# Two-layer hybrid backbone on one core: order ties in retention and feed-forward, and one output row tile moved to SBUF

## The chip, the cores and the metric

The kernel runs on one core of a Trainium2 chip. Five engines work side by side: TensorE (PE in the profile; PEld is its weight load), VectorE (DVE), ScalarE (ACT), GpSimd (POOL) and SyncE (SP), which here only issues DMAs. The metric is the device time of one execution in microseconds; the median of several runs counts.

## The reference, cut to what matters

Two layers work on 512 latent tokens and 256 context tokens of width 1024. Layer 0 is windowed attention plus a SwiGLU feed-forward and is not touched here. Layer 1 is bidirectional retention with four heads, again followed by a feed-forward. For latent tokens, each head computes

```python
q, k = rope_2d(h_x @ w_q), rope_2d(h_x @ w_k)         # 256 columns a head
v, g = h_x @ w_v, h_x @ w_g                           # 512 columns a head
k_c, v_c = h_c @ w_k, h_c @ w_v                       # 256 context tokens
o = retention(q, k, v, k_c, v_c, decay)               # both directions
y = (o - mean(o)) * rsqrt(var(o) + EPS) * gn_gain     # over the head's 512 columns
out += (silu(g) * y) @ w_o
```

and the feed-forward computes `(silu(h @ w_gate) * (h @ w_up)) @ w_out` with 2816 hidden columns.

## The kernel before, in words

**Products in two halves.** Every float32 operand is split into a high part (a cast to the matmul's type, on ScalarE, line 164) and a low part (the rest, on VectorE, line 165). A product is three matmuls: high by high, low by high, high by low. So each weight chunk of 128 x 1024 costs one DMA (lines 122 and 1204), one cast and one subtraction before TensorE can use it. Raw chunks lie in two buffers, `wraw`, or in four wide ones, `wx`.

**Fewer products by sums.** The projections of layer 1 use a seven-product scheme for 2 x 2 blocks. Sums of weight chunks are made on VectorE (lines 1416 to 1420, 1453, 1538 in retention; 903 to 906 in the feed-forward, in `quarter_sums`) or by an accumulating DMA of GpSimd (`add_chunk`, line 1208).

**One retention head.** The loop `for hd in range(RH)` runs: first key products; context keys in PSUM tile `kc` (`context_keys` splits them into `rkc`, lines 1407 to 1411); the query products; `rope_pair` for queries and for keys (lines 1300 to 1311: two products, a sum at line 1307, then a split); value and gate products into the two PSUM banks `Z`; then `scores(m)` for six blocks of 128 keys (lines 1496 to 1515), four latent and two context. A block's score goes to PSUM tile `pj`, is multiplied by the decay strip on VectorE (line 1512, called the shaping here) into `hn`, and is split into `wx`; `accumulate(m)` (lines 1517 to 1522) multiplies it into four PSUM row tiles `ov`, two in the banks `X` and two in the banks `Y`. Each row tile holds 128 tokens by 512 columns. While these run, the gate's weights come in: two weight sums `w1` (line 1538) and two plain chunks `w22` (line 1540). Then every row tile is normalised in place (line 1566), multiplied by the gate (`gated`, line 1572), transposed on TensorE (line 1583) into four tiles in the same banks `X` and `Y`, and copied out with its gain (`turned`, a ScalarE copy at line 1588 and a VectorE low part at line 1589). `out_tile` (line 1619) multiplies by the output weights and adds to the stream.

In head 0 some things differ: in the list `lows` stand the low parts of two weight chunks (`w3`); the casts of two more chunks (`w4`) and the low parts of the context keys are tied behind the last key split (`rope_end`).

In the last head the output is done by halves of 256 tokens. Tokens 256 to 511 (row tiles 2 and 3) are transposed first, the others between output tiles. Squares of the stream are summed there for the second norm, whose logarithm and exponential need another table of ScalarE than the gate's SiLU. `ln_exp_turn()` places that table's load and keeps it as `turn["pre"]`. `second_norm` makes the feed-forward's operand `hx`; `first_weights` brings in its first weights (lines 1643 and 1644).

**The feed-forward.** Hidden tiles come one by one, numbered `f`. The first three are made plainly, the others by `seven`. After the first tile of every group, `output` multiplies the group before by its output weights: one PSUM tile `pj` (of two) for each of eight column blocks, added to the stream on VectorE (line 256). `first_adds` holds the first two of these additions, `copies` the ScalarE copies of the last `seven` (lines 1745 and 1747).

**What sets the order.** Instructions are ordered for each engine when the program is built, by a list scheduler with its own estimate of times and with program order as priority. `after(ins, others)` adds an edge that only this scheduler sees: `ins` is placed after `others`, with no wait on the chip. On the chip each engine takes its instructions in the order so fixed, and waits in place for the data of the next one.

Of the kernel before, what the change touches and what calls it, by code (L numbers as in the profile page):

```python
# [49 lines left out]
def dit_kernel(ctx, tc, xT, cT, crow, small, consts, masks, tabs0, tabs1, jtab, adaQ, adaN, adaT, wst, out):  # L50
    nc = tc.nc
# [610 lines left out]
    vt = []  # L662
# [236 lines left out]

    def quarter_sums(g, u, behind=()):  # L900
# [4 lines left out]
        nc.vector.tensor_tensor(u[:, r_], u[:, r_], g[:, l_], op=sub)  # L905
        nc.vector.tensor_tensor(g[:, r_], g[:, r_], u[:, r_], op=sub)
# [393 lines left out]
    def rope_pair(o, cos1, sin1, behind=()):  # L1300

        res = []
        for op, f0, f1 in ((sub, cos1, sin1), (add, sin1, cos1)):
            a, b = t_hn(SX), t_sq(SX)
            after(nc.vector.tensor_tensor(a, o[0], f0, op=mult), behind)
            after(nc.vector.tensor_tensor(b, o[1], f1, op=mult), behind)
            rope_sum[0] = nc.vector.tensor_tensor(a, a, b, op=op)
# [58 lines left out]
    for hd in range(RH):  # L1366
# [93 lines left out]
        else:  # L1460
# [7 lines left out]
            qh = rope_pair(qt, cos1, sin1, ready)  # L1468
            for low in lows:
                after(low, rope_sum)  # L1470
        kh = rope_pair(kt, cos1, sin1)
        while strip_sums:
            after(strip_sums.pop(), rope_sum)
        if hd == 0:
            context_keys()
        gate = [T(qa, 512, "gate", 4) for _ in range(4)]
# [6 lines left out]
        if hd == 0:  # L1483
            w4 = [split_chunk(v, rope_end) for v in v11]

        def last_values(t):
# [9 lines left out]
        def scores(m):  # L1496
# [3 lines left out]
            v = T(qw, 1024, "wx", 4, F32R)  # L1500
            after(split(vt[m], v[:, 0:512], v[:, 512:]), [] if hd else rope_end)
            so = pj()
# [8 lines left out]
            dec_ap = dx[:, 384 - 128 * mm:896 - 128 * mm] if s == 0 else dcx[:, 128 - 128 * mm:640 - 128 * mm]  # L1511
            nc.vector.scalar_tensor_tensor(sd, so, 1.0 / 16.0, dec_ap, mult, mult)
            ss = T(qw, 1024, "wx", 4, F32R)
# [3 lines left out]
        def accumulate(m, v, sc):  # L1517
            for n in range(4):
# [3 lines left out]
                nc.tensor.matmul(ov[n], sc[1][:, ns], v[0], start=False, stop=m == 5)  # L1522

        pend = scores(0)
        if hd == 0:
# [10 lines left out]
        for i in range(2):  # L1536
            g, v = chunk(bg + i), chunk(bv + i)
            after(nc.vector.tensor_tensor(g, g, v, op=add), [] if hd else rope_end)
            w1.append(split_chunk(g))
        w22 = [split_chunk(chunk(bg + 2 + i)) for i in range(2)]  # L1540
        Zg = [W4("Z"), W4("Z")]
# [23 lines left out]
        for n in (2, 3, 0, 1):  # L1565
            nc.vector.tensor_scalar(ov[n], ov[n], mv[:, 2 * n:2 * n + 1], r[:, n:n + 1], op0=sub, op1=mult)
        if not last:
# [91 lines left out]
        for i, c in ((0, HALVES[1]), (1, HALVES[0])):  # L1659
            for d in range(KT):  # L1660
                ins = out_tile(d, c, "XY" if i else "jZ")
                add_square(0, d, xr[d], c, eng=(nc.vector, nc.gpsimd)[i], fresh=i == 0)
                if (i, d) == (0, 3):
                    transposes(0)
                    turned(HALVES[0])
                if (i, d) in ((0, 5), (0, 7)):
                    first_weights(wx_parts)
# [7 lines left out]
        for i in (5, 7):  # L1675
            weights_end = first_weights(hW_parts, done[i:i + 1])

    norm_end, first_end, first_mult, first_adds = [], [], [], []
# [49 lines left out]
    def seven(late=()):  # L1728
# [5 lines left out]
        split(u[:, 512:1024], *b22, norm_end)  # L1734
        quarter_sums(g, u, first_end[1:2])
        split(u, *b32, first_adds)
        after(split(g, *b14, first_adds), late)
        X, Y, Z = (T(psF, 512, n, 2)[:, 0:SC] for n in "XYZ")
# [219 lines left out]
```

## Time and profile before

| | us |
|---|---|
| median of 3 runs | 1730.82 |
| lowest and highest run | 1728.46, 1735.26 |
| profiled execution, its own time | 1730.99 |
| span of its trace | 1729.2 |
| retention of head 0, from its first products (window 877 to 1002) | 125.0, of which PE busy 123.2 |
| head 1 (1002 to 1125) | 123.0, PE busy 122.4 |
| head 2 (1125 to 1248) | 123.0, PE busy 122.4 |
| head 3, up to the feed-forward (1248 to 1386) | 138.0, PE busy 136.5 |
| feed-forward of layer 1 (1386 to 1729.2) | 343.2, PE busy 337.3 |

Times in the trace count from the start of the span. A timeline row gives start, duration, engine, line, operation, what is written and read, shapes, count, and in brackets the idle time of the engine before it with what ended that. The view of waits sums these brackets by instruction and releaser. A matmul's end in the trace is modelled, so its duration (0.39 us for 512 columns) overlaps the next one's start.

### The profile page before, as it was taken

Reading aid. Unit: us, or ns where it says so; the run is one execution under the profiler, and the core shown is the slowest. Engines: PE = TensorE matmul, PEld = TensorE weight load, DVE = VectorE, ACT = ScalarE, POOL = GpSimd, SP = SyncE. Lnnn points to the kernel's source line nnn. Section 1 sums busy time; section 2 is a strip of 40 time slices with the busy share of each in tenths; the row PEclk is TensorE's granted clock in tenths of the full one; section 3 lists DMA queues with packets and bytes.
Section 4 is the critical chain, followed back from the end, with each engine's and each line's share of the span. In section 5 each row is a group of like instructions: output and inputs, shape, how many; then the busy total and the mean of one; then the engine's idle time right before and its main releaser. Section 6 shows DMA issues by size and latency. Waiting matters only on the chain.

```text
span 1729.2 us, 27806 instructions
## 1 busy us (share of the span) xinstructions
PE 1698.0 (98%) x10876; PEld 1514.3 (88%) x10876; DVE 1341.3 (78%) x2418; ACT 867.5 (50%) x1550; POOL 65.8 (4%) x186
## 2 busy tenths in 40 slices
PE   7999999999999999999999999999999999999999
PEld 5888877899999999999988788898898899899998
DVE  6698889798778788787889757757757798877874
ACT  5587779565433334342555534534525564445442
POOL 0000000000000000000000000000000000000000
PEclk9999999999999999999999999999999999999999
DMA  9612221633253534343543634625624323333322
GB/s 348 241 30 57 62 62 56 207 132 125 74 151 119 157 110 148 122 150 105 152 128 77 193 88 124 179 65 136 183 62 122 98 74 105 115 104 116 99 86 86
DMA packets 63379, 209.58 MB, mean 121 GB/s; under 512 B 7312, under 2 KB 8976, under 8 KB 62992
## 3 DMA queue, kind: packets, MB, share of 16 engines
q1 hardware_dynamic: 53168, 171.63, 31.1%
q0 software_dynamic: 9792, 35.66, 8.3%
q8 instruction: 85, 1.39, 0.3%
q10 hardware_dynamic: 288, 0.52, 0.1%
q14 instruction: 46, 0.38, 0.1%
HBM read 201.75 MB, written 2.10 MB: 118 GB/s over the span
## 4 chain that ended last, share of the span: by engine, by line
PE 81%; DVE 9%; DMA 5%; ACT 3%; issue 2%; SPq 0%; DVEq 0%; ACTq 0%
PE Y L897 14%; PE Z L897 7%; PE pj L147 7%; PE pj L149 7%; PE pj L148 7%; PE Z L1296 5%; PE Y L1285 3%; PE X L897 3%; DMA wraw<-in_wst_dram 3%; PE pj L1296 3%; PE pT L736 2%; PE pO L750 2%; PE S L710 2%; DVE wlo L165 2%; PE X L1285 2%
## 5 line engine op out<-in xcount | busy, mean ns | idle before, releaser
L164 ACT CAST whi<-wraw 128x1024 fp32r<-128x1024 f32 x264 | 276.5, 1051 | 344.4 <-PE Z L149 81.6
L165 DVE TENSOR_TENSOR wlo<-wraw,whi 128x1024 fp32r<-128x1024 f32 x264 | 321.7, 1221 | 80.0 <-ACT whi L164 78.7
L897 PE MATMUL Y<-aq,whi 128*128 128x384 f32 x640 | 173.5, 335 | 0.3 <-ACT hn L1053 0.2
L897 PEld LDWEIGHTS Y<-aq,whi 128*128 128x128 f32 x640 | 116.5, 188 | 1.7 <-ACT hn L1053 1.6
L256 DVE SCALAR_TENSOR_TENSOR res<-pj,mod,res 128x512 f32<-128x512 f32 (+1 forms) x112 | 81.0, 728 | 41.2 <-PE pj L149 41.0
L897 PE MATMUL Y<-aq,wlo 128*128 128x384 f32 x320 | 106.9, 334 | 0.0
L273 DVE CUSTOM_DVE_ANT_0 y<-adaw,crow,small_sb 128x1024 bf16<-128x1024 f32 x64 | 81.9, 1280 | 30.3 <-DMA adaw<-in_adaT_dram 30.0
L1296 PE MATMUL Z<-whi,sA 128*128 128x512 f32 x256 | 80.9, 391 | 0.0
L101 ACT ACTIVATE pr<-pr,stat,qs 128x513 f32<-128x513 f32 (+2 forms) x96 | 74.2, 775 | 9.1 <-DVE stat L717 8.8
L147 PE MATMUL pj<-ax,whi 128*128 128x512 f32 x176 | 69.1, 393 | 1.1 <-DVE res L256 0.9
L149 PE MATMUL pj<-ax,whi 128*128 128x512 f32 x176 | 68.7, 390 | 0.0
L148 PE MATMUL pj<-ax,wlo 128*128 128x512 f32 x176 | 68.6, 390 | 0.0
L147 PE MATMUL pj<-act,whi 128*128 128x512 f32 x168 | 65.6, 391 | 0.0
L148 PE MATMUL pj<-act,wlo 128*128 128x512 f32 x168 | 65.6, 390 | 0.0
L149 PE MATMUL pj<-act,whi 128*128 128x512 f32 x168 | 65.5, 391 | 0.0
L897 PEld LDWEIGHTS Y<-aq,wlo 128*128 128x128 f32 x320 | 60.1, 188 | 0.0
L711 DVE CUSTOM_DVE_ANT_0 pr<-S,mask,qs 128x256 f32<-128x256 f32 (+1 forms) x96 | 53.1, 567 | 7.9 <-PE S L710 5.3
L897 PE MATMUL Y<-sA,whi 128*128 128x256 f32 x304 | 58.1, 277 | 0.6 <-ACT res L1747 0.6
L1296 PEld LDWEIGHTS Z<-whi,sA 128*128 128x128 f32 x256 | 48.0, 188 | 10.4
L897 PE MATMUL Y<-hx,whi 128*128 128x256 f32 x304 | 56.3, 277 | 0.0
L736 PE MATMUL pT<-const_sb,pr 128*128 128x128 f32 x352 | 53.6, 278 | 1.4 <-ACT tt L738 0.9
L1296 PE MATMUL Z<-wlo,sA 128*128 128x512 f32 x128 | 50.4, 394 | 0.7 <-DVE wlo L165 0.7
(578 smaller groups left out, 5049.4 us busy)
## 6 DMA issues: line engine op xcount, KB each, us to landing
wraw<-in_wst_dram SPq DMA_DIRECT2D x224, 512.0 KB, 3.6
adaw<-in_adaT_dram POOLq DMA_DIRECT2D x48, 512.0 KB, 3.9
adan<-in_adaQ_dram SPq DMA_DIRECT2D x16, 512.0 KB, 8.8
wx<-in_wst_dram SPq DMA_DIRECT2D x16, 512.0 KB, 5.7
adan<-in_adaN_dram SPq DMA_DIRECT2D x12, 512.0 KB, 7.8
wx<-in_wst_dram POOLq DMA_DIRECT2D x12, 512.0 KB, 8.4
adaw<-in_adaT_dram SPq DMA_DIRECT2D x8, 512.0 KB, 4.1
wraw<-in_wst_dram POOLq DMA_DIRECT2D x8, 512.0 KB, 5.5
```

The source lines that it names most:

```text
L101: ins = nc.scalar.activation(*args, **kw)
L147: nc.tensor.matmul(o, whi, xhi, start=first, stop=False)
L148: nc.tensor.matmul(o, wlo, xhi, start=False, stop=False)
L149: return nc.tensor.matmul(o, whi, xlo, start=False, stop=last)
L164: after(nc.scalar.copy(hi, t), behind)
L165: return nc.vector.tensor_tensor(lo, t, hi, op=sub)
L256: return nc.vector.scalar_tensor_tensor(res[d], o, mods[l, s][:, part, d:d + 1], res[d], mult, add)
L273: res.append(nc.vector.tensor_tensor_reduce(junk, w, cr[:, s * 1024:(s + 1) * 1024], 1.0, sm_t[:, C_ADAB + l * 48 + j:C_ADAB + l * 48 + j ...
L736: nc.tensor.transpose(tp[:, a * P:(a + 1) * P], self.pr[(0, 2, 1, 3)[a]][:, ki * P:(ki + 1) * P], ident)
L897: nc.tensor.matmul(o, p, r, start=first and k + i == 0, stop=k == 3 and i == 2, skip_group_check=not first)
L1285: ins = nc.tensor.matmul(o[:, e * SC:(e + 1) * SC], p[:, ws], r, start=first and k + e + i == 0, stop=k == 3 and i == 2, skip_group_check= ...
L1296: ins = nc.tensor.matmul(os[t], p, r, start=first and k + i == 0, stop=k == 3 and i == 2, skip_group_check=by_k or not first)
```

## The change

Nothing is computed differently. Apart from one tile, only edges for the scheduler change:

1. `rope_sum` keeps the last two rope sums instead of the last. In head 0 the first low part of `w3` is tied behind the first sum of the queries, the second behind the second; before, both were tied behind the second.
2. In head 0 `context_keys()` is called behind the split of `w4`, and the low parts of the value tiles in `scores` are tied behind the last low part of `w4` (`v_end`) instead of the last key split.
3. In heads 1 to 3 the second weight sum of `w1` is tied behind the second shaping (`sds[1]`). It had no tie.
4. In head 0 the cast of the second `w22` chunk is tied behind the sixth shaping (`sds[5]`). It had no tie.
5. In the last head row tile 1 is normalised into an SBUF tile `hn` and no longer in place in its bank `X`.
6. In the last head the load of the logarithm's table is tied behind the eighth ScalarE copy of `turned`.
7. The two low parts of `first_weights(hW_parts, ...)` are tied behind the last `second_norm` of the first half.
8. In the feed-forward the third sum of `quarter_sums` is tied behind the first addition to the stream (this matters for `f` = 3), and for `f` = 5 the cast of `b14` is tied behind the copy of line 1747 that the tile before makes.

```diff
-            rope_sum[0] = nc.vector.tensor_tensor(a, a, b, op=op)
+            rope_sum[:] = [nc.vector.tensor_tensor(a, a, b, op=op)] + rope_sum[:1]
...
-            for low in lows:
-                after(low, rope_sum)
+            for low, ins in zip(lows, rope_sum[1::-1]):
+                after(low, [ins])
...
-        if hd == 0:
-            context_keys()
         gate = [T(qa, 512, "gate", 4) for _ in range(4)]
...
             w4 = [split_chunk(v, rope_end) for v in v11]
+            v_end = last_split[:]
+            context_keys()
...
-            after(split(vt[m], v[:, 0:512], v[:, 512:]), [] if hd else rope_end)
+            after(split(vt[m], v[:, 0:512], v[:, 512:]), [] if hd else v_end)
...
-            nc.vector.scalar_tensor_tensor(sd, so, 1.0 / 16.0, dec_ap, mult, mult)
+            sds.append(nc.vector.scalar_tensor_tensor(sd, so, 1.0 / 16.0, dec_ap, mult, mult))
...
-            after(nc.vector.tensor_tensor(g, g, v, op=add), [] if hd else rope_end)
+            after(nc.vector.tensor_tensor(g, g, v, op=add), sds[i:2 * i] if hd else rope_end)
             w1.append(split_chunk(g))
-        w22 = [split_chunk(chunk(bg + 2 + i)) for i in range(2)]
+        w22 = [split_chunk(chunk(bg + 2 + i), [] if hd or not i else sds[5:]) for i in range(2)]
...
         for n in (2, 3, 0, 1):
-            nc.vector.tensor_scalar(ov[n], ov[n], mv[:, 2 * n:2 * n + 1], r[:, n:n + 1], op0=sub, op1=mult)
+            raw = ov[n]
+            if last and n == 1:
+                ov[n] = t_hn(512)
+            nc.vector.tensor_scalar(ov[n], raw, mv[:, 2 * n:2 * n + 1], r[:, n:n + 1], op0=sub, op1=mult)
...
                     turned(HALVES[0])
+                    after(turn["pre"], turns[7:8])
...
             weights_end = first_weights(hW_parts, done[i:i + 1])
+            after(weights_end, done[-1:])
...
-        nc.vector.tensor_tensor(u[:, r_], u[:, r_], g[:, l_], op=sub)
+        after(nc.vector.tensor_tensor(u[:, r_], u[:, r_], g[:, l_], op=sub), later)
...
-        quarter_sums(g, u, first_end[1:2])
+        quarter_sums(g, u, first_end[1:2], first_adds[:1])
         split(u, *b32, first_adds)
-        after(split(g, *b14, first_adds), late)
+        after(split(g, *b14, first_adds + (copies[1:2] if f == 5 else [])), late)
```

More of the change, by code (lines that the diff above doesn't have):

```diff
@@ L898, in product, with quarter_sums @@
                                  skip_group_check=not first)
-    def quarter_sums(g, u, behind=()):
+    def quarter_sums(g, u, behind=(), later=()):
         l_, r_ = slice(0, 512), slice(512, 1024)
@@ L1468, in dit_kernel @@
             qh = rope_pair(qt, cos1, sin1, ready)
-            for low in lows:
-                after(low, rope_sum)
+            for low, ins in zip(lows, rope_sum[1::-1]):
+                after(low, [ins])
         kh = rope_pair(kt, cos1, sin1)
         while strip_sums:
-            after(strip_sums.pop(), rope_sum)
-        if hd == 0:
-            context_keys()
+            after(strip_sums.pop(), rope_sum[:1])
         gate = [T(qa, 512, "gate", 4) for _ in range(4)]
@@ L1522, in accumulate @@
                 nc.tensor.matmul(ov[n], sc[1][:, ns], v[0], start=False, stop=m == 5)
+        sds = []
         pend = scores(0)
```

## The prediction, made before the changed kernel ran

> **What bounds the kernel now.** I read the page's first part, then the view of TensorE's waits from 860 us to the end, which holds all of retention and the second feed-forward, then the timelines around each wait.
>
> ```profile
> span 1729.2 us, 27806 instructions
> ...
> PE 1698.0 (98%) x10876; PEld 1514.3 (88%) x10876; DVE 1341.3 (78%) x2418; ACT 867.5 (50%) x1550; POOL 65.8 (4%) x186
> ```
> ```profile
> PE X L1522 <- DVE wx L165: 1.7, 3, 0.6
> PE Z L1296 <- DVE wlo L165: 1.2, 2, 0.7
> PE pj L147 <- DVE res L256: 0.9, 2, 0.8
> PE Y L897 <- ACT res L1747: 0.6, 1, 0.6
> PE X L1520 <- ACT wx L164: 0.6, 1, 0.6
> PE pj L147 <- ACT qk L1588: 0.5, 1, 0.5
> PE X L1583 <- DVE gate L1572: 0.5, 1, 0.5
> PE X L149 <- DVE hx L246: 0.3, 1, 0.3
> ```
>
> TensorE is busy for 98% of the span, so only its own stalls can be won. The edits remove no TensorE work. In the region they touch, the eight rows add up to 6.3 us in 12 waits (total, times, longest). Every row is in a place that an edit touches.
>
> A wait costs more than its bracket. The rows around the first one:
>
> ```profile
> 1083.79 0.40 PE L1521 MATMUL X<-wx 128*128 128x512 f32 x1
> 1084.80 0.50 PE L1522 MATMUL X<-wx 128*128 128x512 f32 x1 [0.61 <-DVE wx L165]
> 1085.13 0.40 PE L1520 MATMUL X<-wx 128*128 128x512 f32 x1
> 1085.37 0.40 PE L1521 MATMUL X<-wx 128*128 128x512 f32 x1
> ```
>
> Undisturbed starts are 0.24 us apart (1085.13 to 1085.37). Here 1.01 and 0.33 pass, that is 0.77 and 0.09 too much: 0.86 us lost for a bracket of 0.61, or 0.25 on top of each wait. Eleven of the twelve waits can be addressed (of the two on L256 the second, some 0.1 to 0.2 us, comes in a later output). The ceiling is 6.3 - 0.2 + 11 x 0.25 = 8.9 us, half a per cent. By the recorded brackets alone it would be 6.1.
>
> **The change part by part.** No DMA, matmul or table load is added or removed. What moves is the order on VectorE and ScalarE. So each price is the wait that goes, less what becomes late next.
>
> *The weight sum behind the second shaping (heads 1 to 3).*
>
> ```profile
> 1080.51 1.23 DVE L1538 TENSOR_TENSOR wraw<-wraw 128x1024 f32<-128x1024 f32 x1 [1.35 <-DMA wraw<-in_wst_dram]
> 1081.66 0.68 DVE L1512 SCALAR_TENSOR_TENSOR hn<-pj,dx 128x512 f32<-128x512 f32 x1
> ...
> 1084.06 0.68 DVE L165 TENSOR_TENSOR wx<-hn,wx 128x512 fp32r<-128x512 f32 x1
> ...
> 1087.51 0.68 DVE L165 TENSOR_TENSOR wx<-hn,wx 128x512 fp32r<-128x512 f32 x1
> ```
>
> VectorE waits 1.35 us in place for a weight chunk, while the shaping behind it could use that time: the sum takes its 1.23 and the shaping starts at 1081.66. With the tie, the shaping goes into the idle 1.35 us, at about 1079.4, and the sum stays at 1080.51, because its DMA sets that. The low part (1084.06) can follow at about 1082.3, well ahead of the matmul that waits until 1084.80. What is behind the sum keeps its place. Late next is the following block's low part, done at 1088.19. Its matmul is the 18th after the waiting one (10 left here, 6 of a score, 2 more): 1084.80 + 18 x 0.24 = 1089.1, a lead of 0.9 us, so head 1 may give back 0.1 to 0.3. Gross 1.7 + 3 x 0.25 = 2.5; I take 2.3. Bounds: 0 if the cast keeps its old place in ScalarE's order, 2.9 if the short late starts next to these waits go too.
>
> *The `w22` cast behind the sixth shaping (head 0).*
>
> ```profile
> 972.70 1.23 DVE L165 TENSOR_TENSOR wlo<-wraw,whi 128x1024 fp32r<-128x1024 f32 x1 [0.71 <-ACT whi L164]
> ...
> 974.44 0.68 DVE L1512 SCALAR_TENSOR_TENSOR hn<-pj,dcx 128x512 f32<-128x512 f32 x1
> ```
>
> The last shaping stands behind 0.71 us of idle time and a chunk's low part that waited for its cast. With the cast held back, the low part moves behind the shaping, which starts up to 1.7 us sooner (974.44 less 972.70). That covers the bracket of 0.55 to 0.6 (row X L1520) and its 0.25; a second late start just behind adds 0.2. I take 1.0, bounds 0.3 and 1.1. The moved low part is late by some 2 us. Its product comes behind the last accumulation and `w1`'s product (12 + 24 matmuls of 0.24 us, 8.6 us), which hide that. On SP's queue the load that takes over its raw buffer, a chunk of the next head, slips as much, with those behind it in the queue; the next head's first products come later still. Without that cover TensorE would lose the 2 us.
>
> *Chunk lows sooner, context keys later (head 0).*
>
> ```profile
> 937.07 0.68 DVE L1307 TENSOR_TENSOR hn<-hn,sq 128x512 f32<-128x512 f32 x1
> ...
> 939.48 0.68 DVE L1307 TENSOR_TENSOR hn<-hn,sq 128x512 f32<-128x512 f32 x1
> 940.08 2.35 DVE L165 TENSOR_TENSOR wlo<-wx,whi 128x1024 fp32r<-128x1024 f32 x2
> ```
> ```profile
> 948.72 0.42 DVE L165 TENSOR_TENSOR rkc<-X,rkc 128x256 fp32r<-128x256 f32 x1
> 949.05 0.68 DVE L165 TENSOR_TENSOR wx<-res,wx 128x512 fp32r<-128x512 f32 x1
> 949.65 1.22 DVE L165 TENSOR_TENSOR wlo<-wraw,whi 128x1024 fp32r<-128x1024 f32 x1
> ```
>
> The first low part moves from 940.08 to about 937.7, which removes the wait of 0.7 in row Z L1296. But here VectorE has no free time: each low part takes 1.13 us from start to start, and pushes the ropes behind it by as much; the key splits that TensorE needs next come no sooner. So most of this gain is waited for again at the scores. What lasts is the second part: context key and value tile step aside, and `wlo` starts at 948.72 instead of 949.65, 0.93 us sooner; half a microsecond more where ScalarE's cast is ready sooner. I take 0.9 for both together; bounds -0.5 (a context or value split that is then late itself) and 1.7 (both brackets, 1.2 + 2 x 0.25).
>
> *One row tile in SBUF and the table load (last head).*
>
> ```profile
> 1352.62 1.53 DVE L1566 TENSOR_SCALAR X<-X,y 128x512 f32<-128x512 f32 x2
> ...
> 1361.45 0.69 DVE L1572 TENSOR_TENSOR gate<-X,gate 128x512 f32<-128x512 f32 x1 [0.70 <-ACT gate L107]
> ```
> ```profile
> 1361.43 1.28 ACT L96 ACT_TABLE_LOAD   x1
> 1362.73 0.84 ACT L1588 ACTIVATE qk<-X,small_sb 128x256 fp32r<-128x256 f32 x2
> ...
> 1369.28 0.47 ACT L1588 ACTIVATE qk<-Y,small_sb 128x256 fp32r<-128x256 f32 x1
> ...
> 1378.14 0.47 ACT L101 ACTIVATE y<-pj,small_sb 128x256 f32<-128x256 f32 x1
> ```
>
> Both banks `X` hold row tiles until the gate products have read them, the last until 1362.14; transposes of the first half need that bank. With row tile 1 in SBUF, its bank is free when the second normalisation ends, 1354.15, eight microseconds sooner. The normalisation itself stays at about its 0.8 us, well ahead of its reader, so the move costs nothing. The copies of `turned` stand behind the load of 1.28 us; with the tie they run before it. Both brackets go, 0.5 each with 0.25 each: 1.5; I take 1.3, bounds 0.3 (only one goes) and 1.5. The load then follows 1369.75, and its first user is at 1378.14, so 8.4 us cover 1.28. The squares of the stream queue behind it meanwhile; if they were late to the end, 1.28 us would be lost there.
>
> The Trainium skill ("ScalarE: Activation LUTs", What ACT_TABLE_LOAD costs) speaks against this tie: a load of about 1.28 us is followed by a drain of about 1.38. In this trace the next copy starts 1.30 us after the load's start, so the drain isn't seen, and the trace decides. By the page the squares would be late by 2.7 us instead of 1.3, and the sum below would lose up to 1.4 us.
>
> *The first weights behind the last norm.*
>
> ```profile
> 1389.50 1.22 DVE L1644 TENSOR_TENSOR wlo<-wraw,whi 128x1024 fp32r<-128x1024 f32 x1
> 1390.64 0.87 DVE L246 SCALAR_TENSOR_TENSOR hx<-hm,mod,hx 128x256 fp32r<-128x256 f32 x2
> 1391.43 1.21 DVE L1644 TENSOR_TENSOR wlo<-wraw,whi 128x1024 fp32r<-128x1024 f32 x1
> ```
> ```profile
> 1389.62 0.51 ACT L245 ACTIVATE hx<-hm,mod 128x256 fp32r<-128x256 f32 x1 [0.21 <-DVE hm L242]
> ```
> ```profile
> 1392.89 0.28 PE L148 MATMUL Y<-hx,wlo 128*128 128x256 f32 x1
> ```
>
> The two `hx` parts come forward by 0.5 to 1.1 us and the wait of 0.3 + 0.25 goes. But the last one needs ScalarE until 1390.13, so it ends at 1390.6; then come both weight parts, 1.13 apart, and the second ends near 1392.9. TensorE, ahead by 0.5, wants it at 1392.4: a new wait of 0.5 takes the old one's place. I take -0.1, bounds -0.5 and 0.55.
>
> *The two ties in the feed-forward.*
>
> ```profile
> 1421.51 0.69 DVE L905 TENSOR_TENSOR wraw<-wraw 128x512 f32<-128x512 f32 x1
> ...
> 1422.84 1.41 DVE L256 SCALAR_TENSOR_TENSOR res<-pj,mod,res 128x512 f32<-128x512 f32 x2
> ```
> ```profile
> 1445.56 2.26 ACT L164 CAST whi<-wraw 128x1024 fp32r<-128x1024 f32 x2 [0.38 <-DVE wraw L905]
> ```
>
> The first output tile's matmuls are done when the third sum starts; the addition that frees its bank stands behind two sums and moves up by their 1.33 us, which covers its wait of 0.8. The third sum slips by 0.6 and the cast of `b32` with it; between it and its product lie the six other output tiles (36 matmuls of 0.24 us, 8.6 us). For `f` = 5 two casts fill ScalarE from 1445.56 to 1447.82 and the copy TensorE waits for comes behind both; with the tie it comes behind the first, 0.95 us sooner, more than its wait of 0.6. Together 0.8 + 0.6 + 2 x 0.25 = 1.9; I take 1.8, bounds 0.8 and 2.0.
>
> **Sum.** 2.3 + 1.0 + 0.9 + 1.3 - 0.1 + 1.8 = 7.2 us. TensorE will then reach the places where another engine is next in line sooner; for these I take off a tenth, 0.7. From the profiled execution's own 1730.99, which lies 0.17 above the median, that gives 1730.99 - 6.5 = 1724.5 us, 0.37% less.
>
> **The rivals.**
>
> *Nothing is late next.* All eleven waits go and the short late starts beside them too: 1730.99 - 8.9 = 1722.1, or some 0.5 less. For it: the edits sit on exactly these rows. Against it: at 937 to 952 us VectorE has no idle time to give, and in the first-weights step a new wait is due.
>
> *The gain moves on.* TensorE runs ahead in heads 0 to 3, but waits again at weights whose chunks come through two raw buffers, so half or more is given back: only the feed-forward and the last head last, 1.8 + 1.3 = 3.1, giving 1727.9. Against it: no row of the wait view names a DMA as TensorE's releaser after 860 us.
>
> *A weight sum in front of a shaping, and the time is longer.* The order is rebuilt from estimated times, and VectorE takes it as it comes. Where a sum is placed ahead of a shaping, TensorE pays for the sum's DMA, as in the quoted 1.35 + 1.23. The first sum of each head has no new tie. If freed places let it slip ahead of the first shaping, each of four heads pays about 2.6 us, 10.4 in all, and the head's gains (2.3 + 1.0 + 0.9) are lost: 1730.99 + 10.4 - 3.0 = 1738.4. It ends slower from the point where a slip costs over 0.75 us a head. Against it: the first sum's load waits for the low parts of `w4`, and those stay ahead of it in data.
>
> *The ties bind nothing.* If the rebuilt order has the pairs already as tied, 1731 remains. Against it: each quoted row shows the opposite order.
>
> **How the numbers follow.** A difference of 0.5% (8.65 us, the limits 1722.2 and 1739.5) is about what a measurement of this kernel can tell from no change. My forecast gets 0.54, nothing late next 0.25, the gain that moves on 0.12, the sum in front 0.07, the ties that bind nothing 0.02. Nearly all of the second case is past 1722.2, and a little of the forecast's spread; most of the fourth is past no limit by itself but its price is uncertain upward. That makes 0.27 faster, 0.67 same, 0.06 slower. The range is 1720.5 to 1730.5: below, all waits with the runs' own scatter of some 2 us; above, the gain that moves on, again with scatter.
>
> **What would show it.** The rows X L1522, X L1520, Y L897 and X L1583 gone from the wait view; the second shaping of heads 1 to 3 ahead of the second weight sum, with the sum's wait for its DMA shorter by the shaping; the load of the table behind the last copy of `turned`; one wait left on Z L1296 or on `qk` near 947 us; a new one on `wlo` near 1392. I am wrong if TensorE's brackets after 860 us still add up to more than 3 us, or if a new row names a DMA or a shaping.

## The result, and the profile after

| | before | after |
|---|---|---|
| median, first comparison (7 runs each) | 1731.44 us (1728.46 to 1736.88) | 1724.84 us (1722.73 to 1726.26) |
| ratio, 95% interval | | 0.9956 (0.9941 to 0.997) |
| median, later, beside three variants on one chip (9 and 5 runs) | 1733.16 us | 1726.43 us |
| ratio, 95% interval | | 0.9962 (0.9949 to 0.9974) |
| profiled execution, its own time | 1730.99 us | 1725.47 us |

The change makes the kernel some 0.4% faster: 6.6 us in the first comparison, 6.7 in the second, and neither interval holds 1. 1724.5 was predicted. First the page of the changed kernel, its span and its busy times, then the view of TensorE's waits from 860 us on.

```profile
span 1723.7 us, 27805 instructions
...
PE 1697.5 (98%) x10876; PEld 1514.5 (88%) x10876; DVE 1341.2 (78%) x2418; ACT 867.9 (50%) x1550; POOL 65.7 (4%) x186
```
```profile
PE pj L147 <- DVE res L256: 0.9, 3, 0.4
PE X L1522 <- DVE wx L165: 0.5, 2, 0.3
PE Z L1296 <- DVE wlo L165: 0.5, 1, 0.5
PE X L149 <- DVE hx L246: 0.3, 1, 0.3
```

The work is the same; 6.3 us of brackets became 2.2, and no row names a DMA or a shaping, so neither sign of being wrong that the prediction gave is there. The rows X L1520, Y L897, `qk` L1588 and X L1583 are gone. What is left on X L1522 is another wait than before: 0.3 and 0.2 us, one block later. In the rows of the changed kernel the lines are a few higher: 1538 is 1539 there, 1566 is 1570, 1583 is 1587, 1588 is 1592, 1644 is 1648, 1747 is 1753.

**A second way to read it** carries the rest of this document. TensorE executes the same number of matmuls in every variant, so the start of the n-th matmul can be compared between two traces. The table gives for each trace how much longer (+) or shorter (-) than in the trace of before TensorE took between the same two matmuls, in us. The columns are stretches of the trace of before: to 930 us nothing is edited; 930 to 960 is head 0 with its ropes and first scores, 960 to 990 its `w22`, 990 to 1075 its end, then heads 1, 2 and 3 up to the last accumulation, the last head's end (to 1388), the first weights (to 1406), the two ties of the feed-forward (to 1452), and what follows. Only the first two rows are the changed kernel; the others are the experiments below.

| trace | to 930 | 960 | 990 | 1075 | head 1 | head 2 | head 3 | 1388 | 1406 | 1452 | 1490 | end |
|---|---|---|---|---|---|---|---|---|---|---|---|---|
| after | -0.35 | -0.83 | -0.90 | 0.03 | -0.63 | -0.52 | -0.67 | -1.56 | 0.52 | -1.76 | 0.56 | 0.59 |
| after, second profile | -0.06 | -0.83 | -1.12 | 0.03 | -0.46 | -0.77 | -0.35 | -1.58 | 0.32 | -1.76 | 0.20 | -0.17 |
| part 1 undone | 0.24 | **-0.57** | -1.12 | 0.02 | -0.77 | -0.62 | -0.58 | -1.61 | 0.37 | -1.78 | -0.78 | -0.03 |
| part 2 undone | 0.84 | **-0.23** | -0.83 | 0.03 | -0.59 | -0.30 | -0.11 | -1.59 | 0.42 | -1.76 | -0.76 | 0.75 |
| part 3 undone | -0.28 | -0.81 | -1.12 | 0.03 | **0.31** | **-0.02** | **1.14** | -1.69 | 0.29 | -1.77 | -0.60 | 0.01 |
| part 4 undone | -0.08 | -0.82 | **0.04** | 1.42 | -0.42 | -0.47 | -0.13 | -1.58 | 0.49 | -1.76 | -0.60 | 0.75 |
| part 5 undone | -0.05 | -0.83 | -1.12 | 0.03 | -0.38 | -0.62 | -0.05 | **0.06** | **0.91** | -1.63 | -0.90 | 0.51 |
| part 6 undone | -0.56 | -0.81 | -1.12 | 1.91 | -0.80 | -0.82 | -0.27 | **-1.72** | 0.35 | -1.64 | -0.26 | 0.79 |
| part 7 undone | -1.11 | -0.80 | -1.12 | 0.01 | -0.53 | -0.69 | -0.30 | -1.61 | **-0.21** | -1.76 | -0.93 | 0.02 |
| part 7 undone, second profile | -1.71 | -0.78 | -0.95 | 1.37 | -0.53 | -0.24 | -0.55 | -1.57 | **-0.26** | -1.76 | 0.53 | -0.27 |
| part 8 undone | -0.95 | -0.80 | -1.12 | 0.09 | -0.77 | -0.49 | -0.43 | -1.59 | 0.32 | **0.02** | 0.64 | 0.77 |
| 7 undone, `w22` tied | -0.00 | -0.84 | -0.87 | 0.09 | **-1.23** | **-1.05** | **-0.75** | -1.56 | -0.26 | -1.58 | -0.01 | -0.18 |
| the same, both lows tied | -0.25 | **-1.02** | -1.12 | 0.67 | -1.23 | -1.05 | -0.21 | -1.57 | -0.26 | -1.75 | 0.63 | -0.13 |

Read down a column, and it shows its own scatter: where no part that works there is undone or added, 960, 1388 and 1452 repeat to some 0.05 to 0.2 us, 990 to 0.3, the heads to 0.4 to 0.6; the first column, which nothing touches, spreads over 2.5 us, and 1075, 1490 and the end over 1 to 2. So one execution's total can't tell a tie of 0.5 us, but a column that repeats this well can; in the heads it takes more than 0.6. The edited columns add up to -6.35 us in the first profile of the changed kernel and -6.55 in the second.

What the shaping tie did, on VectorE in head 1 of the changed kernel:

```profile
1077.34 0.69 DVE L1512 SCALAR_TENSOR_TENSOR hn<-pj,dx 128x512 f32<-128x512 f32 x1 [0.27 <-PE pj L1509]
1078.49 1.23 DVE L1539 TENSOR_TENSOR wraw<-wraw 128x1024 f32<-128x1024 f32 x1 [0.47 <-DMA wraw<-in_wst_dram]
...
1084.33 1.22 DVE L165 TENSOR_TENSOR wlo<-wraw,whi 128x1024 fp32r<-128x1024 f32 x1 [1.06 <-ACT whi L164]
1085.47 0.68 DVE L165 TENSOR_TENSOR wx<-hn,wx 128x512 fp32r<-128x512 f32 x1
```

The shaping now stands ahead of the sum and takes most of the idle time in front of it (0.47 us left of 1.35). One block later a chunk's low part (1084.33) stands in front of the score's low part. It waits for ScalarE:

```profile
1083.25 1.05 ACT L164 CAST whi<-wraw 128x1024 fp32r<-128x1024 f32 x1 [1.93 <-DMA wraw<-in_wst_dram]
1084.21 0.61 ACT L164 CAST wx<-hn 128x512 fp32r<-128x512 f32 x1
```
```profile
1085.53 0.39 PE L1521 MATMUL X<-wx 128*128 128x512 f32 x1
1086.21 0.50 PE L1522 MATMUL X<-wx 128*128 128x512 f32 x1 [0.30 <-DVE wx L165]
```

This cast is the first of `w22`: ScalarE waits 1.93 us in place for its DMA, with the score's cast behind it, and TensorE waits 0.30 for what follows. That is what the head gives back.

### The profile page after: what moved, and what is told of

Same layout as the page of the kernel before. It is cut to its first block, busy times and chain, and to the rows that moved or that the text cites. A ratio compares the mean times of both kernels' runs of the same rounds, so it can differ in the third digit from the quotient of the medians.

```text
span 1723.7 us, 27805 instructions
## 1 busy us (share of the span) xinstructions
PE 1697.5 (98%) x10876; PEld 1514.5 (88%) x10876; DVE 1341.2 (78%) x2418; ACT 867.9 (50%) x1550; POOL 65.7 (4%) x186
## 4 chain that ended last, share of the span: by engine, by line
PE 85%; DVE 6%; DMA 6%; ACT 2%; issue 1%; SPq 0%; DVEq 0%; ACTq 0%
PE Y L897 14%; PE Z L897 7%; PE pj L147 7%; PE pj L149 7%; PE pj L148 7%; PE Z L1296 6%; PE Y L1285 3%; PE X L897 3%; DMA wraw<-in_wst_dram 3%; PE pj L1296 3%; PE pT L736 2%; PE pO L750 2%; PE S L710 2%; PE X L1285 2%; PE X L149 1%; PE X L147 1%
## 5 line engine op out<-in xcount | busy, mean ns | idle before, releaser
L897 PE MATMUL Y<-aq,whi 128*128 128x384 f32 x640 | 173.6, 335 | 0.2 <-ACT hn L1053 0.2
L897 PEld LDWEIGHTS Y<-aq,whi 128*128 128x128 f32 x640 | 116.6, 188 | 1.7 <-ACT hn L1053 1.4
L256 DVE SCALAR_TENSOR_TENSOR res<-pj,mod,res 128x512 f32<-128x512 f32 (+1 forms) x112 | 81.1, 728 | 39.6 <-PE pj L149 39.2
L897 PE MATMUL Y<-aq,wlo 128*128 128x384 f32 x320 | 107.0, 334 | 0.0
L147 PE MATMUL pj<-ax,whi 128*128 128x512 f32 x176 | 69.2, 393 | 0.9 <-DVE res L256 0.9
L147 PE MATMUL pj<-act,whi 128*128 128x512 f32 x168 | 65.6, 390 | 0.0
L897 PEld LDWEIGHTS Y<-aq,wlo 128*128 128x128 f32 x320 | 60.1, 188 | 0.0
L897 PE MATMUL Y<-sA,whi 128*128 128x256 f32 x304 | 58.1, 277 | 0.0
L897 PE MATMUL Y<-hx,whi 128*128 128x256 f32 x304 | 56.3, 277 | 0.0
```

What stands on the lines that cost most here:

```text
L147: nc.tensor.matmul(o, whi, xhi, start=first, stop=False)
L256: return nc.vector.scalar_tensor_tensor(res[d], o, mods[l, s][:, part, d:d + 1], res[d], mult, add)
L897: nc.tensor.matmul(o, p, r, start=first and k + i == 0, stop=k == 3 and i == 2, skip_group_check=not first)
```

## The experiments

Each one is the changed kernel with one edit (the last two have several), read by its column of the table and by its waits. The eight with one part undone ran once each, in 1722.1 to 1727.9 us, with the kernel of before at 1733.9 and 1734.4 beside them; totals of single runs are not used below.

**Part 3 undone** (the second weight sum without its tie).

```diff
-            after(nc.vector.tensor_tensor(g, g, v, op=add), sds[i:2 * i] if hd else rope_end)
+            after(nc.vector.tensor_tensor(g, g, v, op=add), [] if hd else rope_end)
```

> The changed kernel with part 3 undone: in heads 1 to 3 the second weight sum has no tie again. My theory: the second shaping stands behind the sum's wait for its DMA again, and the wait X L1522 <- wx of about 0.6 us comes back in each of the three heads. Measured by the start of the same TensorE instruction in both traces, each head loses 0.8 to 1.2 us at about 1085, 1208 and 1331 us and gains 0.1 to 0.6 back within the next 3 us, where the changed kernel waits at the block after (0.30, 0.24). Net 1.8 us over the three heads, 1727.3 us in all. Rival, the gain moves on: what the tie gains is waited for later at the next chunks, so undoing it costs under 0.6 us by 1345 us. Second rival, the give-back of 0.1 to 0.6 has nothing to do with the tie: then the loss is the full 3.0 us.

The three heads took 0.31, -0.02 and 1.14 us against before, while the changed kernel's two profiles average -0.55, -0.65 and -0.51: the tie is worth 0.9 + 0.6 + 1.65 = 3.1 us, more than the 1.6 to 1.8 that before and after differ by. TensorE's timeline in head 1 of this run:

```profile
1081.50 0.50 PE L1520 MATMUL X<-wx 128*128 128x512 f32 x1 [0.25 <-ACT wx L164]
1082.85 0.50 PE L1522 MATMUL X<-wx 128*128 128x512 f32 x1 [0.61 <-DVE wx L165]
```

The old wait of 0.61 is back, and in front of it a wait for the score's cast that before had no bracket. Before, that start was late too, though the view of waits has no bracket for it:

```profile
1083.04 0.39 PE L1509 MATMUL pj<-qk 128*128 128x512 f32 x1
1083.45 0.50 PE L1520 MATMUL X<-wx 128*128 128x512 f32 x1
```

From 1083.04 to 1083.79 (the next start, shown in the prediction) 0.75 us pass where two steps of 0.227 would make 0.45. So the place cost 0.30 us ahead of the wait, 1.2 in all, and not only the 0.86 of the prediction. Head 3 has the same pair of waits with 0.43 and 0.61. In the changed kernel's first profile the give-back is 0.6, 0.5 and 0.15 us in the three heads, in the second 0.8, 0.3 and 0.5. So the first expectation (a loss with a give-back) holds as a mechanism, but its net of 1.8 us is too small: ahead of the give-back the three heads lose 1.4, 1.0 and 1.6 us, where it named 0.8 to 1.2 each. The net of 3.1 is the second rival's number, but not by its mechanism: the give-back is there.

**Part 7 undone** (the feed-forward's first low parts without the tie behind the last norm).

```diff
             weights_end = first_weights(hW_parts, done[i:i + 1])
-            after(weights_end, done[-1:])
```

> The changed kernel with part 7 undone: the first of the two low parts of the first feed-forward weights goes ahead of the last two hx parts again. Theory A, the tie costs: VectorE's low parts run sooner, and TensorE gains 0.3 to 0.4 us by 1394 us, 1725.1 us in all. Theory B, VectorE's queue as a whole sets it: two hx parts and two low parts have to be done by then in either order and end at the same 1387.2 us, so TensorE waits for hx instead of for wlo (0.25 in the brackets) and the start of the first product by the second wlo moves by under 0.15 us either way. Theory C, the tie helps as it was drawn: 0.3 to 0.5 us lost.

Theory A held: TensorE gains 0.33 us by 1394 us, as it named, and another 0.4 by 1398. Undone, the stretch takes -0.21 us against before, with the tie 0.52 and 0.32. The tie costs 0.5 to 0.8 us. First VectorE with the tie, then without it, and after each the load queue of SyncE:

```profile
1384.44 0.48 DVE L246 SCALAR_TENSOR_TENSOR hx<-hm,mod,hx 128x256 fp32r<-128x256 f32 x1 [0.18 <-ACT hx L245]
1384.85 2.35 DVE L1648 TENSOR_TENSOR wlo<-wraw,whi 128x1024 fp32r<-128x1024 f32 x2
```
```profile
1386.13 1.43 SPq L122 DMA_DIRECT2D wraw<-in_wst_dram  x2
```
```profile
1383.10 1.21 DVE L1648 TENSOR_TENSOR wlo<-wraw,whi 128x1024 fp32r<-128x1024 f32 x1
1384.24 0.87 DVE L246 SCALAR_TENSOR_TENSOR hx<-hm,mod,hx 128x256 fp32r<-128x256 f32 x2
1385.03 1.21 DVE L1648 TENSOR_TENSOR wlo<-wraw,whi 128x1024 fp32r<-128x1024 f32 x1
```
```profile
1384.34 2.25 SPq L122 DMA_DIRECT2D wraw<-in_wst_dram  x2
```

TensorE is 0.71 us earlier in the second trace just before this place. On one clock the first low part therefore runs 1384.85 - (1383.10 + 0.71) = 1.0 us later with the tie. It is the last reader of its raw buffer, so the next load goes out 1386.13 - (1384.34 + 0.71) = 1.1 us later too, and its cast, which stands in front of `hx` casts on ScalarE, starts 1.2 us later (1389.78 against 1387.87 + 0.71). TensorE's timeline with the tie shows both ends of it:

```profile
1386.86 0.28 PE L147 MATMUL Y<-hx,whi 128*128 128x256 f32 x1
1387.25 0.39 PE L148 MATMUL Y<-hx,wlo 128*128 128x256 f32 x1
```
```profile
1397.32 0.38 PE L149 MATMUL X<-hx,wx 128*128 128x256 f32 x1 [0.26 <-DVE hx L246]
```

0.39 us pass to 1387.25 where 0.11 would, because `wlo` ends at 1387.20; ten microseconds on, TensorE waits for `hx`. Without the tie neither wait is there, nor the old one that the tie was put in against.

**Part 5 undone** (row tile 1 in its PSUM bank).

```diff
-            if last and n == 1:
+            if False:
                 ov[n] = t_hn(512)
```

> The changed kernel with part 5 undone: in the last head row tile 1 is normalised in place in its PSUM bank again; the tie of the table's load stays. My prediction's step gave each of the two edits of the last head one wait of 0.5 with 0.25 on top. By it the transposes wait for the gate product again (X L1587 <- gate, 0.5) and 0.75 us of the 1.45 measured in the last head are lost, about 1726.2 us. Rival, the tile makes all of it: without the free bank the transposes come 8 us later, the copies and the load tied behind them too, and all 1.45 us go, or more (up to 1.28 further) if the load then is late for the squares of the stream.

**Part 6 undone** (the table's load without its tie).

```diff
                     turned(HALVES[0])
-                    after(turn["pre"], turns[7:8])
```

> The changed kernel with part 6 undone: the table's load has no tie to the copies of turned; row tile 1 stays in SBUF. My prediction's step: the load goes ahead of copies again, TensorE waits some 0.5 us at pj L147 <- qk, and 0.75 us of the last head's 1.45 are lost, about 1726.2 us. Rival, the tile makes all of it: with the transposes 8 us sooner the copies behind a load of 1.28 us are still early, no wait on qk returns, and the start of the same TensorE instruction at 1376 us moves by under 0.2 us.

The rival held in both: the tile makes the whole gain of the last head. With the tile in its bank and the load still tied, the stretch to 1388 takes 0.06 us against before, 1.6 more than the changed kernel, and three waits stand in its view:

```profile
PE Y L148 <- DVE wlo L1648: 0.5, 1, 0.5
...
PE X L1587 <- DVE gate L1576: 0.5, 1, 0.5
PE pj L147 <- ACT qk L1592: 0.5, 1, 0.5
```

The first row lies among the first weights, which take 0.4 to 0.6 us more here as well. The wait for `qk`, which I had put down to the table's load, comes back although the load (at 1366.70 in this trace) stands behind the copies. The copy that is waited for, at 1359.65, itself waited 1.25 us for a transpose (`X` L1587). So the wait belonged to the transposes, and so to the bank. With the load free and the tile in SBUF, the stretch takes -1.72, and the load goes in between the copies without harm. ScalarE in this run:

```profile
1360.95 1.28 ACT L96 ACT_TABLE_LOAD   x1
1362.25 0.42 ACT L210 ACTIVATE y<-res 128x256 f32<-128x256 f32 x1
...
1363.96 0.84 ACT L1592 ACTIVATE qk<-X,small_sb 128x256 fp32r<-128x256 f32 x2 [0.29 <-PE X L1587]
```

The copies behind it wait for TensorE's transposes, not for the load. So the load's tie is worth nothing once the tile has moved. Whether it would be worth something with the tile in its bank was not tried.

**Part 1 undone** (both low parts behind the second rope sum) **and part 2 undone** (context keys split early, the old tie for the values).

```diff
-            for low, ins in zip(lows, rope_sum[1::-1]):
+            for low, ins in zip(lows, rope_sum[:1] * 2):
```

> The changed kernel with part 1 undone: in head 0 both low parts of w3 stand behind the second rope sum again; parts 2 and 4 stay. My prediction put the lasting gain of parts 1 and 2 together at 0.9 us and said that most of what the sooner low gains is waited for again at the scores, so undoing it should cost at 937 us the wait of 0.7 with 0.25 and by 955 us no more than 0.3 us. Rival: part 1 makes all of the 0.6 us that were measured; then 0.5 us or more are still missing at 969 us.

```diff
+        if hd == 0:
+            context_keys()
         gate = [T(qa, 512, "gate", 4) for _ in range(4)]
...
-            v_end = last_split[:]
-            context_keys()
+            v_end = rope_end
```

> The changed kernel with part 2 undone: in head 0 the context keys are split ahead of the values' weights again, and the value tiles' low parts have the old tie; part 1 stays. My step: wlo is late by 0.9 us again, TensorE waits for it near 949 us, and 0.5 to 0.9 us are lost by 955 us. Rival: with part 1 alone VectorE is far enough ahead, and under 0.2 us are lost.

The stretch to 960 takes -0.57 with part 1 undone and -0.23 with part 2 undone, against -0.83: worth 0.26 and 0.60 us, and they add up to the whole. Against its own place at 935 us TensorE was 0.9 us behind the changed kernel at 940 us without part 1, and 0.24 at 955: the gain is mostly waited for again, as the first expectation had it.

**Part 4 undone** and **part 8 undone**.

```diff
-        w22 = [split_chunk(chunk(bg + 2 + i), [] if hd or not i else sds[5:]) for i in range(2)]
+        w22 = [split_chunk(chunk(bg + 2 + i), []) for i in range(2)]
```

> The changed kernel with part 4 undone: in head 0 the cast of the second w22 chunk has no tie. My step: the wait X L1520 <- wx of 0.5 to 0.6 us near 972 us comes back with 0.25 to 0.5 beside it, 0.8 to 1.1 us lost by 985 us and not given back in the next head. Rival, the gain moves on: the tie lets the next head's first chunk land later, so undoing it gives something back at 980 to 1010 us and the loss at 1010 us is under 0.5 us.

```diff
-        quarter_sums(g, u, first_end[1:2], first_adds[:1])
+        quarter_sums(g, u, first_end[1:2])
...
-        after(split(g, *b14, first_adds + (copies[1:2] if f == 5 else [])), late)
+        after(split(g, *b14, first_adds), late)
```

> The changed kernel with part 8 undone. My step: the wait pj L147 <- res L256 of 0.7 to 0.8 us near 1417 us and the wait Y L897 <- res of 0.6 us near 1440 us come back, and 1.4 to 1.9 us are lost by 1450 us, for the same start of TensorE's instruction. What the changed kernel's profile lost at 1470 to 1478 us (0.38 + 0.23 in the brackets) is open: if it was the price of these ties, it is gone here and the loss by 1500 us is under 0.8 us; if it came from a weight chunk that happened to land late in that one execution, as the last four traces suggest (their cast there waited 0.5 to 0.8 us for its DMA and not 2.1), it is gone here too, but in them as well, and against those the loss stays at 1.4 to 1.9 us up to the end.

In the changed kernel the last shaping of head 0 (line 1512) stands ahead of the chunk's low part, and the first addition (line 256) ahead of the third sum (line 905), both on VectorE. For `f` = 5 the copy (line 1753) stands between the two casts on ScalarE:

```profile
971.73 0.68 DVE L1512 SCALAR_TENSOR_TENSOR hn<-pj,dcx 128x512 f32<-128x512 f32 x1
972.33 1.21 DVE L165 TENSOR_TENSOR wlo<-wraw,whi 128x1024 fp32r<-128x1024 f32 x1
```
```profile
1416.62 0.75 DVE L256 SCALAR_TENSOR_TENSOR res<-pj,mod,res 128x512 f32<-128x512 f32 x1
1417.29 0.68 DVE L905 TENSOR_TENSOR wraw<-wraw 128x512 f32<-128x512 f32 x1
```
```profile
1440.22 1.06 ACT L164 CAST whi<-wraw 128x1024 fp32r<-128x1024 f32 x1 [0.97 <-DVE wraw L905]
1441.18 0.36 ACT L1753 COPY res<-Y 128x256 f32<-128x256 f32 x1
1441.44 1.05 ACT L164 CAST whi<-wraw 128x1024 fp32r<-128x1024 f32 x1
```

Undone, both columns return to zero: 0.04 against -0.90 and -1.12, and 0.02 against -1.76. The old brackets are back, that of `X` L1520 with 0.6 and those of the feed-forward (1400 to 1460 us, part 8 undone):

```profile
PE pj L147 <- DVE res L256: 0.8, 1, 0.8
PE Y L897 <- ACT res L1753: 0.8, 1, 0.8
```

In the trace without part 4 the end of head 0 took 1.42 us more, the opposite of what the rival wanted; the same column shows 1.91 and 1.37 in two kernels that have the tie, so it need not be the tie's doing.

**The changed kernel again, and two variants, in five runs each.** Part 7 undone was timed beside it; to that the first variant adds a tie of the cast found above, and the second also puts both low parts of head 0 behind the first rope sum.

```diff
-            split(sd, ss[:, 0:512], ss[:, 512:])
+            sds_low.append(split(sd, ss[:, 0:512], ss[:, 512:]))
...
-        w22 = [split_chunk(chunk(bg + 2 + i), [] if hd or not i else sds[5:]) for i in range(2)]
+        w22 = [split_chunk(chunk(bg + 2 + i), (sds_low[2:3] if not i else []) if hd else sds[5:] if i else []) for i in range(2)]
```
```diff
-            for low, ins in zip(lows, rope_sum[1::-1]):
+            for low, ins in zip(lows, rope_sum[1:2] * 2):
```

> The changed kernel once more, unedited, as the base of the next three on the same chip and as a second profile of it. If what it lost at 1465 to 1480 us (1.1 to 1.5 us against seven other traces) is the price of an order, it is lost here again; if it was the scatter of one execution, the cast of whi near 1466 us waits about 0.5 to 0.8 us for its DMA and not 2.1, and those waits (L256, 0.38 + 0.23) are gone. Likewise 0.2 us near 968 us.

> Part 7 undone, timed in rounds. Theory from the first look: the tie holds the first low part behind the last hx parts, so its raw buffer comes free 1.2 us later, the next chunk's load goes out 1.2 us later, its cast stands in front of the hx casts on ScalarE, and TensorE loses 0.73 us between 1385 and 1399 us. So 0.7 us less than the unedited kernel on the same chip (0.3 to 1.1 with the scatter of the medians). Rival, scatter: the same within 0.3 us, and the hx wait near 1397 us is there in this profile.

> Part 7 undone, and in heads 1 to 3 the cast of the first w22 chunk tied behind the low part of the third score. What the shaping tie gave and took back in the same head (0.60 and 0.52 us in heads 1 and 2) would be the price of this cast: it waits in place 1.9 us for its DMA, with the score's cast behind it. Theory: the waits X L1522 <- wx (0.30, 0.24) vanish, and 0.6 to 1.1 us are gained over the three heads against part 7 undone alone. Rival, the gain moves on: the chunk held back by 1.3 us delays the next loads through its raw buffer, TensorE waits for w22 or for the next head's first chunks, and the net is 0 or a loss of up to 1 us.

> As before, and in head 0 both low parts of w3 behind the first rope sum. The wait Z L1296 <- wlo of 0.49 us with 0.25 near 942 us goes. My prediction's reading of this place: VectorE has no idle time to give there, so what the low gains is waited for again at the scores, and of 0.7 us at 946 us under 0.3 us are left at 955 us. Rival: 0.5 us or more last; or the later rope sum makes a key or query part late, and it is a loss.

| same chip | median us (lowest to highest) | mean | ratio to before, 95% interval |
|---|---|---|---|
| changed kernel | 1726.43 (1723.61 to 1727.29) | 1725.8 | 0.9962 (0.9949 to 0.9974) |
| part 7 undone | 1724.09 (1722.27 to 1724.63) | 1723.7 | 0.995 (0.9938 to 0.9963) |
| and `w22` tied | 1723.24 (1720.89 to 1724.98) | 1723.3 | 0.9948 (0.9935 to 0.996) |
| and both lows tied | 1723.63 (1722.54 to 1724.19) | 1723.4 | 0.9947 (0.9934 to 0.9961) |

Part 7 undone again takes -0.26 in its stretch (0.32 with the tie, 0.6 apart); the medians lie 2.3 apart, the means 2.0, more than the stretch explains, and with five runs each the rest can't be told from scatter. The wait near 1397 us is missing in the changed kernel's second profile: of the tie's price the wait for `wlo` is there in both, that for `hx` in one.

At 1465 to 1480 us the second profile of the changed kernel lies between the two expectations: the cast waits 1.41 us for its DMA, one bracket of 0.50 is left on L256, and 0.20 us are lost from 1452 to 1490 instead of 0.56. The kernel without the ties of part 8 loses 0.64 there, so the loss is not their price. The 0.2 us near 968 us are gone, so they were scatter.

The tied cast works in its place. The heads take -1.23, -1.05 and -0.75, 1.2 to 1.5 us less in all than the changed kernel's -1.82 and -1.58, and 1.5 to 1.7 less than the two profiles of part 7 undone, more than the 0.6 to 1.1 expected. Nothing is late at the next head. The second trace with this tie (the last row) repeats -1.23 and -1.05, but makes only -0.21 in head 3: up to 1345 us both traces have the same -0.83, then 0.6 us go within four matmuls, without a bracket. Why is open; the first cast of that head's last weights waited 0.97 us for its DMA in this trace and 0.46 in the other. ScalarE in head 1, and all of TensorE's waits from 860 us on, in the first variant:

```profile
1083.64 0.62 ACT L164 CAST wx<-hn 128x512 fp32r<-128x512 f32 x1 [2.03 <-DVE hn L1512]
1084.17 1.05 ACT L164 CAST whi<-wraw 128x1024 fp32r<-128x1024 f32 x1
```
```profile
PE pj L147 <- DVE res L256: 0.2, 1, 0.2
```

The medians of the variants can't be told apart; all three beat the changed kernel's median by 2.3 to 3.2 us, and 0.5% less than before is the best that was reached. With both lows tied the result lies between the two expectations: against the changed kernel 0.63 us are gained from 935 to 943 and 0.41 are left at 955. But this trace had lost 0.2 just before 935, so the stretch to 960 as a whole takes -1.02 and not -0.83, 0.2 better; by that the first expectation, under 0.3, is the nearer one. Part of the gain is paid to a strip that the scores need next:

```profile
946.42 0.47 PE L1507 MATMUL pj<-qk 128*128 128x512 f32 x1 [0.40 <-DVE dcx L1331]
```

## Why the prediction was right

The sum holds as a whole, and three of its terms by their own working:

- **The `w22` cast, 1.0 predicted.** 0.90 and 1.12 measured, all of it gone when undone. The load behind it made nothing late: the next column is 0.03 in both profiles.
- **Chunk lows and context keys, 0.9.** 0.83, in the shares that the step gave: most of the first low's gain is waited for again (0.26 lasts), the second part makes 0.60.
- **The feed-forward ties, 1.8.** 1.76, with 1.78 lost when undone. The bracket plus 0.25 gives the right sum here, where the brackets of before alone make 1.4. How much of it is bracket is less sure: in the trace without the ties the same loss shows 0.8 and 0.8.

Three were off:

- **The weight sum behind the shaping, 2.3.** Gross it is worth more, 3.0: with the give-back tied away the heads make 1.23 + 1.05 + 0.75 in one trace, and up to 1345 us the same in the other, whose head 3 then loses 0.6 elsewhere. The excess over 2.5 is mostly the short late starts ahead of the wait (0.3 us in head 1, 0.1 in head 2), which the bound of 2.9 had named. Net it was 1.6 to 1.8. The step saw the right successor, "the following block's low part", with a lead of 0.9 us, and took off 0.1 to 0.3 for it. It missed that a cast waiting for its DMA stands in front of that block on ScalarE, and its low part in front of it on VectorE: 0.15 to 0.8 us went back in each head, 1.2 to 1.5 in all. The general tenth taken off the sum, 0.7, was about this.
- **The last head, 1.3.** 1.6, and one mechanism instead of two. The row "pj L147 <- ACT qk L1588" named the copies, and a load of 1.28 us stood in front of them, but they were late for the transposes, which waited for the bank. Only undoing each edit by itself showed it.
- **The first weights, -0.1.** -0.3 to -0.5. The new wait on `wlo` came where it was announced. What the step left out is the raw buffer: a low part held back frees it later, and the next load, its cast and the `hx` casts behind it follow. And the wait of 0.3 on `hx` that was to go was gone without the tie: with the last head's edits in place and part 7 undone the stretch shows no wait at all.

Parts measured 6.35 and 6.55 us against 7.2 - 0.7 = 6.5. That agreement is partly luck: too little for the last head, too much for heads 1 to 3 and the first weights, and the deduction covers the difference. The median's distance of 0.3 us from 1724.5 is luck as well: the two profiled spans lie only 5.5 us apart, because stretches that no edit touches were slower by 0.8 in the later one, and the seven runs spread over 3.5.

Of the rivals, "nothing is late next" describes the variant with the tied cast (0.2 us of brackets left) better than the change itself. "The gain moves on" is true inside heads 1 to 3 and of the first low part, but not for half of the whole. The first profile seemed to support it in the feed-forward, where 0.56 us went between 1452 and 1490; but seven other traces gain there, and of the four others that lose 0.2 to 0.64 one has no ties in the feed-forward. No weight sum slipped in front of a first shaping, and every part but 6, when undone, changed what TensorE waits for.

The Trainium skill ("ScalarE: Activation LUTs", What ACT_TABLE_LOAD costs) adds a drain of about 1.38 us to the load of 1.28, without saying on which side of it. In the changed kernel the copy in front ends at 1364.45 and the next cast again starts 1.30 us after the start of the load:

```profile
1364.46 1.28 ACT L96 ACT_TABLE_LOAD   x1
1365.76 1.05 ACT L1647 CAST wx<-wraw 128x1024 fp32r<-128x1024 f32 x1
```

With the load ahead of four of the copies it is 1.30 too (1360.95 to 1362.25, and the cast in front ends at 1360.94), so the page's drain was seen in neither order and on neither side, and TensorE shows no wait for it.

## What to carry to other kernels

Before a tie holds an instruction back, list what that instruction frees as well as what it feeds: a low part of a weight chunk frees the raw buffer, and through it the next load and every cast queued behind that load's cast. Before a wait is put down to the instruction that stands in front of the one named (a table load, a sum), ask what that one itself waits for; two edits at one stall are told apart only by undoing each alone. And where runs scatter by more than an edit is worth, subtract the starts of the same matmuls in two traces: a stretch can repeat to 0.1 us while the total moves by 3.

## What the runs showed of the hardware

**Two paces of the same matmuls.** Matmuls of 256 columns started 0.113 us apart in an undisturbed stretch, but in the first weights of the changed kernel 0.118 apart until 1393.7, with no idle time shown. From TensorE's timeline (five steps, then fourteen):

```profile
1391.83 0.28 PE L147 MATMUL X<-hx,whi 128*128 128x256 f32 x1
...
1392.42 0.28 PE L149 MATMUL Y<-hx,whi 128*128 128x256 f32 x1
...
1393.84 0.28 PE L149 MATMUL Y<-hx,wx 128*128 128x256 f32 x1
...
1395.42 0.28 PE L148 MATMUL X<-hx,wx 128*128 128x256 f32 x1
```

0.59 / 5 = 0.118 and 1.58 / 14 = 0.113. Both profiles of the changed kernel do this. Fifty steps behind the late start at 1387.25 take 5.89 us in them, and 5.71 in both profiles of part 7 undone: 0.18 us, part of what part 7 costs. The late start is not shown to be the cause: the ten starts from 1385.67, ahead of it, are 0.118 apart already, and with part 5 undone, where the same matmul is later still (a bracket of 0.5), the fifty steps take 5.71. What sets the slow pace stays open. The step of 0.24 that the prediction called undisturbed is a slow one as well: most 512-column matmuls in the trace of before start 0.226 or 0.227 us apart.

**One place where runs scatter.** At the end of head 0 the first chunk of the next stage is loaded while GpSimd's accumulating DMAs use the same engines: between 985 and 1000 us in the changed kernel its queue took 48.3% of the 16 DMA engines' time, SyncE's 33.3%. The cast of that chunk in the changed kernel, then in the kernel with part 6 undone, whose order is the same there:

```profile
994.12 1.05 ACT L164 CAST whi<-wraw 128x1024 fp32r<-128x1024 f32 x1 [3.40 <-DMA wraw<-in_wst_dram]
```
```profile
996.98 1.05 ACT L164 CAST whi<-wraw 128x1024 fp32r<-128x1024 f32 x1 [6.68 <-DMA wraw<-in_wst_dram]
```

The DMA landed some 3 us later, the `qk` low parts queue behind that chunk's low part on VectorE, and TensorE lost the 1.9 us in the table's column 1075:

```profile
1001.92 0.50 PE L147 MATMUL X<-qk,whi 128*128 128x512 f32 x1 [1.55 <-DVE qk L1593]
```

Four of the thirteen traces lose 0.7 to 1.9 us there, in kernels of different edits. The Trainium skill ("DMA: Bandwidth & Descriptors", Issuing engines are not separate DMA queues) says that DMAs started by the scalar, sync or gpsimd engine all run on the same 16 DMA engines and interleave there. That agrees with the late landing, but no run here took GpSimd's transfers away to show it. The scatter of the first column and of 1490 was not traced.
